# Rotary embedding on one core: unit 0 loaded by two DMA issuers instead of three, with 24 KB rows on GpSimd

## The chip, the cores and the metric

One core of a Trainium2 chip runs the whole kernel. The metric is the device time of one execution in microseconds (us). A profiled execution also has a span, from the first to the last recorded instruction, some 1.7 us shorter than the time. A run more than 1.5% above the fastest of its kernel is labelled slow.

## The reference

```python
# x: (8, 8, 1024, 64) fp32, freqs: (32,), positions: (1024,), scale = 0.5
angles = np.outer(positions * scale, freqs)
cos, sin = np.cos(angles), np.sin(angles)
x1, x2 = x[..., :32], x[..., 32:]
out = np.concatenate([x1 * cos - x2 * sin, x1 * sin + x2 * cos], axis=-1)
```

16.8 MB come in, 16.8 MB go out, and each output element takes two products and one sum or difference.

## The kernel before

The 64 heads are worked on in 4 units of 16 heads. A unit is a tile of 128 partitions with N = 8192 values each, so one partition's row is 32 KB of fp32 in HBM. In this kernel GpSimd's loads of x cast to fp16 on the way in; those from SyncE and ScalarE do not, so what they load goes into an fp32 tile X0f and ScalarE casts it. NH is N / 2.

```python
X0f = xout.tile([P, N], FP32, tag="O")
Q = NH // 2
pin(nc.sync.dma_start(out=X0f[:, :Q], in_=xv[0][:, NH : NH + Q]))      # third quarter, 8 KB rows

pin(nc.scalar.dma_start(out=pos_i64, in_=...))                         # 128 rows of 64 B
pin(nc.scalar.dma_start(out=freq_row, in_=freqs[None, :]))             # one row of 128 B
pin(nc.scalar.dma_start(out=X0f[:, Q:NH], in_=xv[0][:, NH + Q :]))     # last quarter, 8 KB rows
# ...
pin(nc.gpsimd.dma_start(out=Xf[0][:, :NH], in_=xv[0][:, :NH]))         # first half, 16 KB rows, cast
# ... (constants)
for u in range(1, NU):
    pin(nc.gpsimd.dma_start(out=Xf[u], in_=xv[u]))                     # 32 KB rows, cast
# ... (tables: cfreq and posf -> y -> r -> sine and cosine -> spread to T by TensorE,
#      copied from PSUM by VectorE and ScalarE)
pin(nc.scalar.copy(out=Xf[0][:, NH:], in_=X0f[:, :NH]))                # cast of SyncE's and ScalarE's half

for u in range(NU):
    OUT = xout.tile([P, N], FP32, tag="O")                             # 3 buffers
    for s in range(2):                                                 # two halves of a row
        # ...
        pin(nc.vector.tensor_tensor(out=pr, in0=Xs, in1=sin_b, op=ALU.mult))
        pin(nc.vector.tensor_tensor(out=Xs, in0=Xs, in1=cos_b, op=ALU.mult))
        # ... one subtract and one add on VectorE
        pin(nc.scalar.copy(out=OUT[:, ns], in_=Xf[u][:, ns]))
        if u in (0, NU - 1):
            eng = nc.gpsimd if (u, s) == (0, 1) else nc.sync
            pin(eng.dma_start(out=ov[u][:, ns], in_=OUT[:, ns]))       # half a unit
    if u not in (0, NU - 1):
        pin(nc.gpsimd.dma_start(out=ov[u], in_=OUT))                   # a whole unit
```

## Time and profile before

| | before |
|---|---|
| time, median of the first three runs | 84.3 us (84.08 to 84.32) |
| span of the profiled run | 82.7 us |
| VectorE busy / ScalarE busy | 73% / 49% |
| packets of all DMA queues, share of 16 engines | 96.7% |
| first packet / last packet ends | 1.74 / 81.40 us |

The DMA engines are shared by all queues, and each DMA is cut into one packet for each partition's row, 8 rows an engine. "Packet records" below are the trace's list of such packets, with start, duration and size. In the views q0 is GpSimd's queue, q1 SyncE's and q10 ScalarE's. A bracket at the end of a timeline line gives how long the engine had been idle and what ended the wait. A load has landed when its completion is signalled. The prediction shows the lines and how they are read.

### The profile page before, as it was taken

Reading aid. Unit: us, or ns where it says so; the run is one execution under the profiler, and the core shown is the slowest. Engines: PE = TensorE matmul, PEld = TensorE weight load, DVE = VectorE, ACT = ScalarE, POOL = GpSimd, SP = SyncE. Lnnn points to the kernel's source line nnn. Section 1 sums busy time; section 2 is a strip of 40 time slices with the busy share of each in tenths; the row PEclk is TensorE's granted clock in tenths of the full one; section 3 lists DMA queues with packets and bytes.
Section 4 is the critical chain, followed back from the end, with each engine's and each line's share of the span. In section 5 each row is a group of like instructions: output and inputs, shape, how many; then the busy total and the mean of one; then the engine's idle time right before and its main releaser. Section 6 shows DMA issues by size and latency. Waiting matters only on the chain.

```text
span 82.7 us, 179 instructions
## 1 busy us (share of the span) xinstructions
PE 6.5 (8%) x18; PEld 2.5 (3%) x18; DVE 60.3 (73%) x40; ACT 40.1 (49%) x18; POOL 5.2 (6%) x15
## 2 busy tenths in 40 slices
PE   0020898100000000000000000000000000000000
PEld 0020332000000000000000000000000000000000
DVE  0306376999999999999999999999999997000000
ACT  0603169999950790394098059209606902940000
POOL 4920000000000002000000200000200000000000
PEclk9999999997555555555555555555555555555555
DMA  2899997997997999799998999997999699699990
GB/s 56 328 319 281 285 345 167 254 246 151 238 254 143 238 285 317 285 278 333 262 222 174 278 468 396 507 507 317 444 507 460 301 507 492 285 468 396 436 444 16
DMA packets 1874, 26.22 MB, mean 317 GB/s; under 512 B 338, under 2 KB 338, under 8 KB 338
## 3 DMA queue, kind: packets, MB, share of 16 engines
q0 software_dynamic: 1008, 17.83, 72.0%
q1 hardware_dynamic: 576, 7.34, 21.5%
q10 hardware_dynamic: 290, 1.06, 3.2%
HBM read 16.79 MB, written 16.78 MB: 406 GB/s over the span
## 4 chain that ended last, share of the span: by engine, by line
DVE 55%; ACT 15%; DMA 5%; issue 5%; PE 5%; DVEq 1%; ACTq 0%
DVE X L154 20%; DVE pr L153 19%; DVE X L158 9%; DVE X L155 6%; ACT T L139 6%; DMA freq_row<-in_freqs_dram 5%; ACT OUT L161 4%; PE ps L129 4%; ACT X L140 4%; DVEq L195 1%; PE cfreq L97 1%; ACT tab L122 1%; DVE r L113 1%; DVE y L104 1%; ACTq L69 0%
## 5 line engine op out<-in xcount | busy, mean ns | idle before, releaser
L161 ACT CAST OUT<-X 128x4096 f32<-128x4096 f16 x8 | 28.8, 3606 | 24.2 <-DVE X L158 24.2
L153 DVE TENSOR_TENSOR pr<-X,T 128x4096 f16<-128x4096 f16 x8 | 18.3, 2292 | 1.0 <-ACT T L139 0.7
L154 DVE TENSOR_TENSOR X<-X,T 128x4096 f16<-128x4096 f16 x8 | 18.3, 2292 | 0.3
L155 DVE TENSOR_TENSOR X<-X,pr 128x2048 f16<-128x2048 f16 x8 | 9.8, 1225 | 0.3
L158 DVE TENSOR_TENSOR X<-pr,X 128x2048 f16<-128x2048 f16 x8 | 9.7, 1218 | 0.0
L139 ACT CAST T<-ps 128x1024 f16<-128x1024 f32 x6 | 5.7, 1028 | 2.6 <-PE ps L129 2.6
L129 PE MATMUL ps<-tab,sel 128*128 128x512 f16 x16 | 5.9, 529 | 2.6 <-ACT tab L122 2.2
L137 DVE CAST T<-ps 128x1024 f16<-128x1024 f32 x2 | 2.5, 1225 | 2.2 <-PE ps L129 2.2
L140 ACT CAST X<-X0f 128x4096 f16<-128x4096 f32 x1 | 3.6, 3650 | 0.0
L166 POOL DMA_DIRECT2D out_dram<-OUT x2 | 1.1, 533 | 27.1 <-ACT OUT L161 27.1
L95 DVE COPY sel<-one 128x2048 f16<-128x2048 f16 x1 | 0.7, 693 | 2.8 <-POOL one L87 2.8
L117 ACT ACTIVATE tab<-r 128x256 f16<-128x256 f32 x1 | 0.4, 417 | 4.2 <-DVE r L113 4.2
L117 ACT ACT_TABLE_LOAD x1 | 1.3, 1283 | 2.1 <-issue 2.1
L164 POOL DMA_DIRECT2D out_dram<-OUT x1 | 0.5, 543 | 26.7 <-ACT OUT L161 26.7
L129 PEld LDWEIGHTS <-sel 128*128 128x128 f16 x16 | 2.0, 126 | 6.0 <-issue 5.7
L92 POOL DMA_DIRECT2D X<-in_x_dram x3 | 2.0, 659 | 0.0
L100 DVE CAST posf<-pos_i 128x8 f32<-128x8 int32 x1 | 0.2, 172 | 2.3 <-DMA pos_i<-in_positions_dram 2.3
L97 PE MATMUL cfreq<-freq_row,coef 1*128 1x32 f32 x2 | 0.6, 392 | 5.7 <-DMA freq_row<-in_freqs_dram 5.7
L104 DVE TENSOR_TENSOR y<-posf,cfreq 128x256 f32<-128x256 f32 x1 | 0.4, 422 | 0.4 <-PE cfreq L97 0.4
L83 POOL DMA_DIRECT2D X<-in_x_dram x1 | 0.7, 669 | 0.8 <-POOLq L181 0.8
L97 PEld LDWEIGHTS cfreq<-freq_row,coef 1*128 1x128 f32 x2 | 0.5, 308 | 5.7 <-issue 5.7
L122 ACT ACTIVATE tab<-ra,quarter 128x256 f16<-128x256 f32 x1 | 0.5, 507 | 0.0
(11 smaller groups left out, 2.3 us busy)
## 6 DMA issues: line engine op xcount, KB each, us to landing
out_dram<-OUT POOLq DMA_DIRECT2D x2, 4096.0 KB, 14.9
X<-in_x_dram POOLq DMA_DIRECT2D x3, 2048.0 KB, 31.8
out_dram<-OUT SPq DMA_DIRECT2D x3, 2048.0 KB, 10.5
out_dram<-OUT POOLq DMA_DIRECT2D x1, 2048.0 KB, 21.1
X0f<-in_x_dram SPq DMA_DIRECT2D x1, 1024.0 KB, 4.8
X<-in_x_dram POOLq DMA_DIRECT2D x1, 1024.0 KB, 11.6
X0f<-in_x_dram ACTq DMA_DIRECT2D x1, 1024.0 KB, 12.1
pos_i<-in_positions_dram ACTq DMA_DIRECT2D x1, 8.0 KB, 5.0
```

Of the source, the lines that this page charges most:

```text
L92: pin(nc.gpsimd.dma_start(out=Xf[u], in_=xv[u]))
L97: nc.tensor.matmul(out=cfreq, lhsT=coef, rhs=freq_row, start=True, stop=True)
L117: pin(nc.scalar.activation(out=tab[:, 0], in_=r, func=AF.Sin, bias=0.0, scale=-_TWO_PI_DN))
L129: nc.tensor.matmul(out=ps[:, i].rearrange("p t w -> p (t w)"), lhsT=sel[:, g + i].rearrange("s h q -> s (h q)"), rhs=tab.rearrange("s t k ...
L137: pin(nc.vector.tensor_copy(out=dst, in_=ps))
L139: pin(nc.scalar.copy(out=dst, in_=ps))
L140: pin(nc.scalar.copy(out=Xf[0][:, NH:], in_=X0f[:, :NH]))
L153: pin(nc.vector.tensor_tensor(out=pr, in0=Xs, in1=sin_b, op=ALU.mult))
L154: pin(nc.vector.tensor_tensor(out=Xs, in0=Xs, in1=cos_b, op=ALU.mult))
L155: pin(nc.vector.tensor_tensor(out=Xs[:, :, 0, :], in0=Xs[:, :, 0, :], in1=pr[:, :, 1, :], op=ALU.subtract))
L158: pin(nc.vector.tensor_tensor(out=Xs[:, :, 1, :], in0=pr[:, :, 0, :], in1=Xs[:, :, 1, :], op=ALU.add))
L161: pin(nc.scalar.copy(out=OUT[:, ns], in_=Xf[u][:, ns]))
```

## The change

Its intent: to take bulk loading off ScalarE's queue, so that ScalarE issues only the two small loads, to halve ScalarE's cast, and to give GpSimd longer rows.

```diff
-    Q = NH // 2
-    pin(nc.sync.dma_start(out=X0f[:, :Q], in_=xv[0][:, NH : NH + Q]))
+    Q = N // 4
+    pin(nc.sync.dma_start(out=X0f[:, :Q], in_=xv[0][:, N - Q :]))
...
-    pin(nc.scalar.dma_start(out=X0f[:, Q:NH], in_=xv[0][:, NH + Q :]))
...
-    pin(nc.gpsimd.dma_start(out=Xf[0][:, :NH], in_=xv[0][:, :NH]))
+    pin(nc.gpsimd.dma_start(out=Xf[0][:, : N - Q], in_=xv[0][:, : N - Q]))
...
-    pin(nc.scalar.copy(out=Xf[0][:, NH:], in_=X0f[:, :NH]))
+    pin(nc.scalar.copy(out=Xf[0][:, N - Q :], in_=X0f[:, :Q]))
```

## The prediction

> **What bounds the kernel now.** I read the page first. Its part 1 has VectorE (DVE) as the busiest compute engine at 73%, and its part 4 follows the chain that ended last mostly through VectorE (55%). That is an invitation to count VectorE's waits. Three further lines speak against it:
>
> ```profile
> q0 software_dynamic: 1008, 17.83, 72.0%
> q1 hardware_dynamic: 576, 7.34, 21.5%
> q10 hardware_dynamic: 290, 1.06, 3.2%
> HBM read 16.79 MB, written 16.78 MB: 406 GB/s over the span
> ```
>
> The last column is the time that each queue's packets took, as a share of 16 DMA engines over the whole span. Summed it is 96.7% of 82.7 us, or 79.9 us. No other resource is near that. (The page's own 317 GB/s counts destination bytes, and a load that casts fp32 to fp16 writes half of what it reads; the 33.6 MB through HBM are the real load.)
>
> A mean share can hide gaps, so next comes the view by windows, cut where the DMA work changes. Columns: stretch and length, busy us of PE, PEld, DVE, ACT and POOL, the clock, DMA share, GB/s (destination bytes).
>
> ```profile
> 0.00:1.74 1.74, 0.00 (x0) 0.00 (x0) 0.00 (x0) 0.00 (x0) 0.69 (x5) 1.00 0.00 0
> 1.74:4.70 2.96, 0.00 (x0) 0.00 (x0) 0.69 (x1) 1.28 (x1) 2.86 (x8) 1.00 0.99 346
> 4.70:12.60 7.90, 4.66 (x12) 2.03 (x13) 4.06 (x7) 2.36 (x4) 0.00 (x0) 1.00 1.12 301
> 12.60:22.00 9.40, 1.80 (x7) 0.48 (x5) 8.59 (x5) 9.40 (x7) 0.00 (x0) 0.87 0.99 211
> ...
> 61.50:71.50 10.00, 0.00 (x0) 0.00 (x0) 8.05 (x5) 5.42 (x2) 0.00 (x0) 0.50 1.00 431
> 71.50:81.40 9.90, 0.00 (x0) 0.00 (x0) 0.00 (x0) 1.79 (x1) 0.00 (x0) 0.50 0.93 399
> 81.40:82.70 1.30, 0.00 (x0) 0.00 (x0) 0.00 (x0) 0.00 (x0) 0.00 (x0) 0.50 0.00 0
> ```
>
> The DMA share is about 1 in every stretch between 1.74 and 81.4 (packets are booked where they start, so it wobbles around 1). I also added up the packet records over time: from 4 us to 80 us no stretch of 2 us has less than 15.98 of 16 engines at work. VectorE, on the other hand, does nothing in the last 10 us. The span is therefore three pieces: 1.74 us until the first packet, 79.7 us of packets without a gap, 1.25 us until the last store is confirmed.
>
> How much slack has the compute chain against that? From the timeline and the chain of waits:
>
> ```profile
> 66.31 7.33 SPq L164 DMA_DIRECT2D out_dram<-OUT  x2
> 69.69 3.60 ACT OUT L161
> ```
>
> ScalarE writes the last half output until 73.3, and SyncE starts issuing its store then. By the packet records that store's first packet starts at 75.92, straight behind the last packet of the store before it on the same queue. On an empty queue SyncE's first load took 1.0 us from issue (0.74) to first packet (1.74), so the last store could have started at 74.3. The chain through VectorE and ScalarE is thus some 1.6 us early (an estimate from these two numbers). **The bound is the DMA engines**; the chain in part 4 is only the longest chain of instructions.
>
> **What the Trainium skill says.** "DMA: Bandwidth & Descriptors", section "Issuing engines are not separate DMA queues", says that DMAs started by ScalarE, SyncE or GpSimd all end up on the same 16 DMA engines and interleave. The trace agrees: alone, SyncE's 8 KB rows take 309 ns each; while ScalarE's 8 KB rows and GpSimd's 16 KB rows are both under way, one of each takes 924 ns on an engine, the sum of the two plus about 10 ns. The same page, section "SWDGE vs HWDGE vs iDMA", says that only a DMA from GpSimd can cast. That is why the rows that leave ScalarE's queue also change from fp32 plus a ScalarE cast to a cast in flight. "Perfetto Trace Analysis", section "What 'DMA-bound' means", asks which DMA resource binds: here it is the engines and not an issuing sequencer, whose issues take 0.35 to 0.9 us each. The first page's section "Where 436 GB/s comes from" gives a ceiling of about 435 GB/s; the 33.6 MB in 79.7 us are 421 GB/s, so there is little left to gain from any arrangement of the same bytes.
>
> **The change part by part.** Unit 0 is 128 rows (partitions) of 32 KB in HBM.
>
> ```profile
> 1.25 0.67 POOL L83 DMA_DIRECT2D X<-in_x_dram  x1 [0.81 <-POOLq L181]
> 1.74 0.35 ACTq L72 DMA_DIRECT2D X0f<-in_x_dram  x1
> 13.20 2.29 DVE L153 TENSOR_TENSOR pr<-X,T 128x4096 f16<-128x4096 f16 x1 [0.67 <-ACT T L139]
> 16.68 3.65 ACT L140 CAST X<-X0f 128x4096 f16<-128x4096 f32 x1
> 20.36 2.29 DVE L153 TENSOR_TENSOR pr<-X,T 128x4096 f16<-128x4096 f16 x1 [0.15 <-ACT X L140]
> ...
> X0f<-in_x_dram SPq DMA_DIRECT2D x1, 1024.0 KB, 4.8
> X<-in_x_dram POOLq DMA_DIRECT2D x1, 1024.0 KB, 11.6
> X0f<-in_x_dram ACTq DMA_DIRECT2D x1, 1024.0 KB, 12.1
> ```
>
> *SyncE's load.* Q is 2048 before and after (a quarter of a row, 8 KB). SyncE only takes another quarter, the last instead of the third. Cost and time to landing stay at 4.8 us.
>
> *Bytes on the DMA engines.* HBM bytes do not change. Removed: 128 rows of 8 KB (ScalarE) and 128 of 16 KB (GpSimd); added: 128 of 24 KB (GpSimd). Each engine has 8 of each. Before: 8 x 924 ns = 7.39 us. After: a 16 KB row alone took 605 ns (first GpSimd row at 4.72, first ScalarE row behind it at 5.325) and a 32 KB row of the later units 1208 ns from start to start; halfway between, 24 KB is 906 ns, so 8 x 906 = 7.25 us. The saving is **0.14 us**, on the bound.
>
> *When unit 0 lands.* Before, GpSimd's half landed at 1.25 + 11.6 = 12.85, about 0.54 after its last packet (12.31). Now three quarters land together: packets that ended at 12.61 end 0.14 earlier, at 12.47, and with 0.54 for completion the landing is at about **13.0**. VectorE's first product waits until 13.18 for the tables T, the copy by ScalarE that the trace names. So it should still start near 13.2, with only 0.2 us to spare.
>
> *ScalarE's cast.* L140 shrinks from 4096 to 2048 elements a row: 3.65 to about 1.83 us. It follows the table copies, so it ends near 18.5 instead of 20.33, and VectorE's second half starts when it is free, at 20.23 instead of 20.36: 0.13 us off the compute chain. The other 1.7 us become idle time of ScalarE, because its next work (L161) waits for VectorE at 20.24 either way.
>
> *ScalarE's issue.* One issue of 0.35 us goes; the table load behind it moves up to about 1.75. It had over 4 us to spare before the first sine at 7.59. The two small loads ahead of it are issued as before, and frequencies that land at 5.6 still start the tables.
>
> Sum: the compute chain is about 0.13 us shorter and the DMA stream about 0.14 us shorter. As they lie beside each other, I take the stream: 84.3 - 0.14 = 84.16, put at **84.2 us**.
>
> **The rivals.** (1) *The first product waits for the longer load.* If the single completion for three quarters comes after 13.18, VectorE starts late by the difference. For it: the margin is 0.2 us, and the half of the data that the first product needs is no longer announced on its own. Against a cost: the chain has about 1.6 us to spare at its end, so a landing up to about 14.7 costs nothing; beyond that, each microsecond costs one. Only a landing over 3 us late would reach 2%. (2) *ScalarE's relief pays.* If the chain of part 4 were the bound and the cast on it (4.2% of the span), one would expect up to 1.8 us, so 82.5. Against it: VectorE waited only 0.15 us for this cast, and the stores drain at full rate until 81.4. (3) *Long GpSimd rows run badly*, or delay the small frequency row because a 0.9 us packet gets in front of it. For it: that row's packet (4.84) is near GpSimd's first (4.72). Against it: 32 KB rows already run at 27.1 bytes per ns and engine, as fast as any; a delayed frequency row would cost the chain at most one packet, 0.9 us, inside its slack. A bad row rate of 10% would cost 0.7 us, 85.0. (4) *A hole in the stream*: with one queue fewer at the start an engine might run dry. Against it: GpSimd's queue alone holds share 0.99 between 12.6 and 22.
>
> **Range and chances.** Everything that I can put a number on lies within 0.2 us, and three runs before spread by 0.24. So 83.9 to 84.5 should hold it 8 times in 10; the longer side of what may go wrong is slower. Two per cent is 1.7 us. Faster by that would need bytes to vanish (chance 0.01); slower would need a landing 3 us late or a much worse row rate (0.02); within 2%: 0.97.
>
> **What would show it right or wrong.** Right: DMA shares still sum to 96 to 97% of the span; GpSimd's first load lands about 11.7 us after its issue; VectorE's first product at about 13.2, waiting for T; the L140 cast at 1.8 us and no wait of VectorE for it; the end still 1.2 us after the last packet, with the last store queued behind the one before it. Wrong: a first product waiting on the DMA of X well beyond 13.2, a stretch after 1.74 us with a DMA share well below 1, 24 KB rows far from 906 ns, or an end that follows the last ScalarE cast directly.

## The result, and the profile after

| | before | after |
|---|---|---|
| time, median of 6 runs | 84.27 us (84.08 to 84.33) | 84.17 us (84.08 to 84.44) |
| ratio | | 0.9997, 95% interval 0.9977 to 1.0016 |

A ratio compares the fast runs of both kernels in the same rounds, so it is not quite the ratio of the medians. The profiled run after happened to be the longest of its six (84.44).

First the page after, DMA queues: packets, MB written at the destination, share of 16 engines.

```profile
q0 software_dynamic: 1008, 18.35, 75.3%
q1 hardware_dynamic: 576, 7.34, 21.5%
q10 hardware_dynamic: 146, 0.01, 0.1%
```

ScalarE's queue q10 has given its 3.2% to GpSimd's queue q0. The sum is 96.9%, as full as before. The view by windows, the same columns as in the prediction:

```profile
1.74:4.70 2.96, 0.00 (x0) 0.00 (x0) 0.69 (x1) 1.28 (x1) 2.86 (x8) 1.00 0.98 337
4.70:12.60 7.90, 4.46 (x12) 1.98 (x13) 3.94 (x7) 2.17 (x4) 0.00 (x0) 1.00 1.12 240
...
71.50:81.40 9.90, 0.00 (x0) 0.00 (x0) 0.00 (x0) 1.94 (x1) 0.00 (x0) 0.50 0.96 410
```

The DMA share is near 1 again to the end, with VectorE idle in the last stretch. The fall from 301 to 240 GB/s between 4.7 and 12.6 is no loss: more of the load is cast, and these are destination bytes. By the packet records the 24 KB rows follow each other at 907 ns on an engine (926 ns each, overlapping a little), where a pair of a 16 KB and an 8 KB row took 924 ns before.

The timeline and the DMA issues of unit 0:

```profile
13.39 2.29 DVE L152 TENSOR_TENSOR pr<-X,T 128x4096 f16<-128x4096 f16 x1 [0.67 <-ACT T L138]
16.87 1.94 ACT L139 CAST X<-X0f 128x2048 f16<-128x2048 f32 x1
20.51 2.29 DVE L152 TENSOR_TENSOR pr<-X,T 128x4096 f16<-128x4096 f16 x1
...
X<-in_x_dram POOLq DMA_DIRECT2D x1, 1536.0 KB, 11.4
X0f<-in_x_dram SPq DMA_DIRECT2D x1, 1024.0 KB, 4.7
```

Three quarters of unit 0 now land together at 1.25 + 11.4 = 12.65. The first product still waits for the tables and not for this load. The cast is 1.7 us shorter (1.94 instead of 3.65), and the bracket that told VectorE's wait of 0.15 us for it is gone. All of ScalarE's gain became its idle time: its wait for VectorE rose from 24.2 to 25.8 us in the sum of the output casts.

The tables came 0.2 us later in this profile, since TensorE got the frequencies at 5.91 instead of 5.71. That is not an effect of the change: other profiles of the same lines have 5.59 to 5.77 (below).

### The profile page after: what moved, and what is told of

Same layout as the page of the kernel before. It is cut to its first block, busy times and chain, and to the rows that moved or that the text cites. A ratio compares the mean times of both kernels' runs of the same rounds, so it can differ in the third digit from the quotient of the medians.

```text
span 82.7 us, 177 instructions
## 1 busy us (share of the span) xinstructions
PE 6.7 (8%) x18; PEld 2.7 (3%) x18; DVE 60.3 (73%) x40; ACT 38.5 (47%) x18; POOL 5.2 (6%) x15
## 4 chain that ended last, share of the span: by engine, by line
DVE 64%; ACT 7%; DMA 6%; issue 5%; PE 5%; DVEq 1%; ACTq 0%
DVE X L153 22%; DVE pr L152 22%; DVE X L157 10%; DVE X L154 8%; DMA freq_row<-in_freqs_dram 6%; ACT OUT L160 4%; PE ps L128 4%; DVEq L194 1%; ACT T L138 1%; PE cfreq L96 1%; ACT tab L121 1%; DVE r L112 1%; DVE y L103 1%; ACTq L69 0%; ACT tab L116 0%
## 5 line engine op out<-in xcount | busy, mean ns | idle before, releaser
L160 ACT CAST OUT<-X 128x4096 f32<-128x4096 f16 x8 | 28.8, 3606 | 25.8 <-DVE X L157 25.8
L139 ACT CAST X<-X0f 128x2048 f16<-128x2048 f32 x1 | 1.9, 1942 | 0.0
## 6 DMA issues: line engine op xcount, KB each, us to landing
X<-in_x_dram POOLq DMA_DIRECT2D x1, 1536.0 KB, 11.4
```

Of the source, the lines that this page charges most:

```text
L139: pin(nc.scalar.copy(out=Xf[0][:, N - Q :], in_=X0f[:, :Q]))
```

## The experiments

Two theories. **A**: the DMA engines are the bound; the chain through VectorE and ScalarE ends with time to spare. **B**: that chain sets the end, and the DMA is full only because there is always something to store. All runs start from the changed kernel; ratios are against the kernel before in the same rounds. All results are correct except where a store is cut short.

### The changed kernel again

No edit.

> The changed kernel once more. Both theories: 84.1 to 84.3, ratio to before 0.998 to 1.000 if the 0.14 us saved on the DMA stream survive, 1.000 if they do not. In the profile: rows of 24 KB 907 ns from start to start, first load of GpSimd landing 11.4 us after issue. Open: whether the frequency row is again 0.2 us later than before (5.9 against 5.7).

Measured: 84.22 us (84.03 to 84.56), ratio 0.9992, interval 0.9969 to 1.0014. The 24 KB rows are at 907 ns again and their load lands at 1.25 + 11.5 = 12.75. The frequencies reach TensorE at 5.59, so the 0.2 us of the first profile was scatter. Whether the 0.14 us saved in unit 0 reach the end is below the resolution: they would be 0.17%, and the interval is 0.22% to each side. The packet records show where they drown. In the profile after, unit 1's rows ended 0.15 us earlier than before (22.16 against 22.31), and in the eight profiles that have the changed loads they ended between 22.02 and 22.26. Unit 3's, loaded while SyncE's first store runs among them, ended between 47.08 and 47.62 in these eight (47.27 before).

### VectorE delayed near the end, by a little and by much

```diff
             pin(nc.vector.tensor_tensor(out=pr, in0=Xs, in1=sin_b, op=ALU.mult))
+            if (u, s) == (3, 0):          # a_late1: half a product more
+                h = KH // 2
+                pin(nc.vector.tensor_tensor(out=pr[:, :h], in0=Xs[:, :h], in1=sin_b[:, :h], op=ALU.mult))
```

In a_late5 two whole products stand there instead.

> Half a product more on VectorE at the start of unit 3, idempotent, 1.17 us. Theory A (the DMA stream is the bound, the compute chain has about 1.6 us to spare at the last store): 84.2, no change. Theory B (the chain through VectorE and ScalarE sets the end): 85.3.

Measured: 84.40 us, ratio 1.0003, interval 0.998 to 1.0027. A microsecond of VectorE costs nothing that the time resolves (0.3% is 0.2 us).

> Two whole products more on VectorE at the start of unit 3, 4.6 us. Theory A: 4.6 less the slack of 1.6 to 1.7, so 87.1 (3.0 us slower), with a hole in the DMA stream before the last store. Theory B: 88.8.

Measured: 87.16 us, ratio 1.0334, against 84.32 before: 2.84 us slower for 4.66 us (two repeats of 2.33) of delay, so 1.8 us of slack at the last store. (By the spans, 85.0 to 85.2 against 82.3 to 82.8, the slack would be nearer 2.1 us: in this kernel alone the time is 2.0 us longer than the span and not 1.7 to 1.8, and no run says why.) The windows of that run show the hole between the last two stores:

```profile
71.50:76.50 5.00, 0.00 (x0) 0.00 (x0) 2.67 (x3) 2.27 (x1) 0.00 (x0) 0.50 0.99 419
76.50:78.70 2.20, 0.00 (x0) 0.00 (x0) 0.00 (x0) 1.34 (x1) 0.00 (x0) 0.50 0.02 7
78.70:83.80 5.10, 0.00 (x0) 0.00 (x0) 0.00 (x0) 0.00 (x0) 0.00 (x0) 0.50 0.96 408
```

B falls with these two: it asked for 85.3 and 88.8.

### The same small delay, one unit earlier

The edit of a_late1 with (2, 0) instead of (3, 0).

> The same 1.17 us as in a_late1, but at the start of unit 2, so that GpSimd's store of unit 2 is issued later too (at 60.8 instead of 59.64, while its first packet was at 61.6). Theory A with a GpSimd store that needs 1.0 us from issue to first packet: 84.2 to 84.5. If it needs the whole 1.95 us seen, the slack is nil there: 85.3 and a hole of 1.2 us at 61.6. Theory B: 85.3 too, but without a hole.

Measured: 84.46 us, ratio 1.0011, interval 0.9988 to 1.0035. The time does not tell it from no change, but the trace does. The windows before and inside a short hole (a window counts packets by their starts):

```profile
51.50:61.20 9.70, 0.00 (x0) 0.00 (x0) 9.56 (x6) 5.41 (x2) 0.53 (x1) 0.50 1.00 432
...
61.30:61.70 0.40, 0.00 (x0) 0.00 (x0) 0.37 (x2) 0.00 (x0) 0.00 (x0) 0.50 0.02 0
```

GpSimd issued unit 2's store at 60.64, 1.2 us later than in a_late1, and its first packet came at 61.74, 1.1 us after that. The share of 0.02 alone proves no hole, since rows of unit 1's store that had started before still ran until 61.65. Added up by starts and ends, the packet records show 0.3 us of the 16 engines' time lost here, where a_late1 lost none, and the first packet came 0.37 us later than in a_late1 (61.37). So the slack at unit 2's store is about 0.8 us, half of that at the last store.

### Less to store

Two kernels that are wrong: a_less_tail leaves out a quarter of the row of the store before the last, a_less_mid half of the row of unit 1's store.

```diff
+                if (u, s) == (3, 0):                       # a_less_tail
+                    ns = slice(0, NH - NH // 4)
                 pin(eng.dma_start(out=ov[u][:, ns], in_=OUT[:, ns]))
-            pin(nc.gpsimd.dma_start(out=ov[u], in_=OUT))
+            w = N - N // 2 if u == 1 else N                # a_less_mid
+            pin(nc.gpsimd.dma_start(out=ov[u][:, :w], in_=OUT[:, :w]))
```

> Wrong on purpose: a quarter of the second last store (unit 3, first half) is left out, 4 KB of each row, 8 x 151 ns = 1.2 us of the DMA stream; no instruction of VectorE or ScalarE changes. Theory A: 83.0 (the 1.2 us are under the slack of 1.6 to 1.7). Theory B: 84.2, as the chain is the same.

Measured: 82.95 us against 84.25 before, ratio 0.9837 (0.9808 to 0.9865). Removing 1.2 us of packets removed 1.3 us of time, while no compute instruction changed.

> Wrong on purpose: half of unit 1's store (16 KB of each row, 8 x 605 ns = 4.8 us of the stream) is left out. Theory A, with the slack that a_mid1 showed at unit 2's store (about 0.8 us: 1.17 us late left a hole of 0.33 us): the gain is cut to 0.8 us, 83.4, and a hole of 4 us stands in the stream before unit 2's store. If the slack were the 1.6 us of the last store: 82.6. Theory B: 84.2.

Measured: 83.23 us against 84.12, ratio 0.9921 (0.9866 to 0.9976); three runs at 83.2 to 83.3 and one at 84.2. Of 4.8 us of packets some 0.9 us came through; the rest is a hole before unit 2's store, 3.8 us of the 16 engines' time by the packet records:

```profile
57.10:60.50 3.40, 0.00 (x0) 0.00 (x0) 3.33 (x3) 2.06 (x1) 0.53 (x1) 0.50 0.00 0
60.50:70.50 10.00, 0.00 (x0) 0.00 (x0) 9.01 (x6) 4.46 (x2) 0.00 (x0) 0.50 1.04 446
```

Unit 2's store could not start before 60.55, against 61.37 in a_late1's profile: 0.8 us, the slack that a_mid1 had shown.

### ScalarE's cast made as long as before

```diff
     pin(nc.scalar.copy(out=Xf[0][:, N - Q :], in_=X0f[:, :Q]))
+    pin(nc.scalar.copy(out=Xf[0][:, N - Q :], in_=X0f[:, :Q]))
```

> ScalarE does its cast of X0f twice (idempotent), so that it is busy as long as before the change: 3.9 us. Theory A: VectorE waits 0.1 to 0.3 us for it, 84.2. If ScalarE's relief were worth its length: 86.1.

Measured: 84.26 us, ratio 1.0016, interval 0.9998 to 1.0033. The timeline:

```profile
18.59 1.90 ACT L140 CAST X<-X0f 128x2048 f16<-128x2048 f32 x1
20.40 3.60 ACT L161 CAST OUT<-X 128x4096 f32<-128x4096 f16 x1
20.52 2.29 DVE L153 TENSOR_TENSOR pr<-X,T 128x4096 f16<-128x4096 f16 x1 [0.37 <-ACT X L140]
```

VectorE waits 0.37 us for the cast, inside the slack. ScalarE's relief of 1.7 us is worth nothing that the time resolves.

### Another share for SyncE: an eighth, nothing, a half

`Q = N // 8` in a_eighth; in a_whole the load of SyncE and the cast are removed and GpSimd loads all of unit 0; `Q = N // 2` in a_half.

> SyncE loads only the last eighth of unit 0, GpSimd seven eighths. Theory A: SyncE's packets end near 3.4, GpSimd's first packet comes at 4.7, so the engines are idle for about 1.4 us and the time is 85.5. Theory B: VectorE's first product waits for GpSimd's load at 4.72 + 8 x 1057 ns + 0.25 = 13.4, as now; ScalarE's cast is 1 us shorter: 84.2 or a little less.

Measured: 84.26 us, ratio 1.0007, interval 0.9962 to 1.0052. A's number was wrong. There is no hole, because GpSimd's first row came at 3.50, not at 4.7. I had read 4.7 as GpSimd's own start-up; it was a wait behind SyncE's rows. The first product was now late, at 13.68, since GpSimd's load landed at 1.25 + 12.3 = 13.55, and that too cost nothing that the time resolves:

```profile
13.68 2.29 DVE L152 TENSOR_TENSOR pr<-X,T 128x4096 f16<-128x4096 f16 x1 [2.54 <-ACT T L138]
```

The bracket names a copy of the tables, which had long been written; the load is what landed last.

> GpSimd loads all of unit 0, no load by SyncE, no cast by ScalarE. Theory A: the stream starts at 4.7 instead of 1.75, minus nothing: 87.1. Theory B: unit 0 lands at 4.72 + 8 x 1208 ns + 0.25 = 14.6, 1.3 us after the tables: 85.4.

Measured: 85.02 us, ratio 1.0084 (1.0052 to 1.0115). Both numbers were off for the same reason: with no SyncE load at all, GpSimd's first row came at 2.63. The windows at the start, and the first product:

```profile
1.70:2.60 0.90, 0.11 (x1) 0.14 (x1) 0.00 (x0) 0.89 (x1) 0.82 (x5) 1.00 0.09 9
2.60:12.60 10.00, 6.30 (x18) 2.31 (x18) 4.67 (x8) 5.42 (x8) 2.06 (x4) 1.00 1.05 210
...
13.94 2.29 DVE L148 TENSOR_TENSOR pr<-X,T 128x4096 f16<-128x4096 f16 x1 [4.08 <-DMA X<-in_x_dram]
```

The stream starts 0.88 us late and the time is 0.7 to 0.85 us longer. VectorE starts 0.7 us late as well, so this run alone would not separate A from B; the packets of the last stores still follow each other without a gap, which is A's mark. SyncE's early load is worth these 0.7 to 0.85 us.

> SyncE loads half of unit 0 in one DMA of 16 KB rows, GpSimd the other half; ScalarE loads no x but casts 4096 elements a row again (3.65 us). Theory A: same bytes, no hole: 84.2. Theory B with ScalarE's cast on the path: as before the change, 84.3, VectorE waiting 0.1 to 0.2 us for the cast.

Measured: 88.96 us, ratio 1.0512 (1.0437 to 1.0587). A large miss of both theories. Its profile fell on a run labelled slow (89.37, which is 1.5% above the kernel's fastest, 88.05); the fast runs, 88.05 to 89.33, are all at least 3.8 us slower than before, and the profiled run's clock (0.63) is as theirs. The timeline:

```profile
10.67 0.17 DVE L99 CAST posf<-pos_i 128x8 f32<-128x8 int32 x1 [7.18 <-DMA pos_i<-in_positions_dram]
11.74 0.60 PE L96 MATMUL cfreq<-freq_row,coef 1*128 1x32 f32 x2 [11.74 <-DMA freq_row<-in_freqs_dram]
19.22 2.29 DVE L152 TENSOR_TENSOR pr<-X,T 128x4096 f16<-128x4096 f16 x1 [0.67 <-ACT T L138]
```

The two small loads landed 5 to 6 us late, the tables followed, and the first product started at 19.22 instead of 13.2. That is 6 us, far over the slack, and the DMA share is 0.00 from 62.4 to 66.6, once more before unit 2's store. Added up, the records show 4.3 us of the engines' time lost there and 0.7 us before unit 1's store. The 64 B rows of the positions ran from 2.86 to 9.54 and ended with SyncE's 16 KB rows (1.76 to 9.54). In the changed kernel they end with SyncE's 8 KB rows too (5.12).

### Is it SyncE's row size or SyncE's bytes?

```diff
-    Q = N // 4
-    pin(nc.sync.dma_start(out=X0f[:, :Q], in_=xv[0][:, N - Q :]))
+    Q = N // 2
+    h = Q // 2
+    pin(nc.sync.dma_start(out=X0f[:, :h], in_=xv[0][:, N - Q : N - h]))
+    pin(nc.sync.dma_start(out=X0f[:, h:Q], in_=xv[0][:, N - h :]))
```

> SyncE loads the same half of unit 0 as in a_half, but as two DMAs of 8 KB rows instead of one of 16 KB rows. In a_half (4.7 us slower) the positions landed at 10.7 and the frequencies at 11.7 us instead of 5.7, and the tables came 6 us late. Theory C (on each DMA engine the 64 B rows of ScalarE's small loads alternate one for one with SyncE's rows, so SyncE's row size sets when they land): positions at 5.7 to 6.0 again, first product at 13.2 to 13.5, time 84.2. Theory D (the small loads wait until SyncE's bytes are through, or 2 MB ahead of them are simply too much): as a_half, first product near 19, 88 to 89.

Measured: 84.10 us, ratio 1.0000 (0.9985 to 1.0014).

```profile
5.64 0.60 PE L98 MATMUL cfreq<-freq_row,coef 1*128 1x32 f32 x2 [5.64 <-DMA freq_row<-in_freqs_dram]
5.78 0.17 DVE L101 CAST posf<-pos_i 128x8 f32<-128x8 int32 x1 [2.30 <-DMA pos_i<-in_positions_dram]
13.13 2.29 DVE L154 TENSOR_TENSOR pr<-X,T 128x4096 f16<-128x4096 f16 x1 [0.67 <-ACT T L140]
```

The same 2 MB on the same queue, in rows of half the size, cost nothing. Theory D falls, and the size of SyncE's first eight rows an engine is what sets when the small loads land. Every load of SyncE here has eight rows an engine, so the times alone do not part the row's size from the whole first load's; the packet records do, with one 64 B row an engine after each of SyncE's rows (every 0.31 us in the changed kernel, every 0.61 us at first in a_half).

The next run asks whether the turns really alternate. In a_freq1st ScalarE issues the frequencies first and the positions second.

> ScalarE issues the frequency row ahead of the positions. Theory C: the frequencies then take their turn after the first row of SyncE and land before 4 us; the positions still need eight turns and land at 5.7 to 6.2, so the tables start within 0.4 us of now. Theory A: whatever it is, 84.2, for the chain has slack.

Measured: 84.31 us, ratio 1.0019 (0.9998 to 1.0039), with one slow run, 85.45, on which the profile fell. In that profile SyncE's rows run from 1.75 to 5.01, much as in the fast runs (1.75 to 5.12 in the profile after).

```profile
2.17 0.63 PE L96 MATMUL cfreq<-freq_row,coef 1*128 1x32 f32 x2 [2.17 <-POOL quarter L84]
5.63 0.17 DVE L99 CAST posf<-pos_i 128x8 f32<-128x8 int32 x1 [2.13 <-DMA pos_i<-in_positions_dram]
```

The frequencies had arrived before TensorE was ready for them at 2.17, and the positions by 5.63. The times are near Theory C's, but not by its mechanism: the frequency row went out at 1.62, before SyncE's first row and not after it. The positions, issued 0.55 us later than otherwise, took no turns between SyncE's rows: all their packets lie between 4.75 and 5.07, when SyncE's were almost through. Alternation is what the packets show when both loads are issued at once; a load issued a little later waits behind rows that the engines seem to have taken in already. What rule joins the two stays open.

## Why the prediction was right

*The bound.* Right, and tested from both sides: 1.2 us less to store gave 1.3 us, while 1.2 us more on VectorE gave nothing that the time resolves. After the change, too, the last store's first packet (76.13) came right behind the last rows of the store before it, and the end 1.2 us after the last packet (81.44). No run separates the 16 engines from the memory behind them as what sets the rate of a row. Part 4 of the page, which follows waits between instructions, could not show this; the sum of the queues' shares could.

*The saving of 0.14 us.* Its term is right: 907 ns for each 24 KB row where 906 was worked out, and unit 1's loads ended 0.15 us earlier. At the end of the kernel it is not resolved, and I do not claim it for the time; that the median came to 84.17 where 84.16 was worked out is luck within a spread of 0.36 us.

*Unit 0's landing.* 12.65 instead of the 13.0 expected. I had taken 0.54 us from last packet to landing from the kernel before; here it was 0.25. The records show what I misread: the load ends with 16 packets of 4 B, and before the change these took turns with ScalarE's last rows, the last of them at 12.61, 0.24 us before the landing. The tables of that profile were ready at 13.37, so the margin was 0.7 us and not 0.2; in a_again, with 12.75 against 13.06, it was 0.3.

*ScalarE's cast.* 1.94 us where 1.83 was estimated by halving, and VectorE's wait for it gone, as expected. a_cast2 shows that nothing was to be had there.

*The slack, the mis-sized term.* "The chain is some 1.6 us early" holds for the last store (1.8 measured; in a_late5 that store needed 0.8 us and not 1.0 from issue at 77.87 to first packet at 78.70). But a delay at the start of the kernel, the only one that this change could cause, also delays unit 2's store, and there only 0.8 us are free. (Unit 1's store, though earlier, has more: in a_half 6 us of delay left a hole of 0.7 us there.) The rival's sentence that a landing "up to about 14.7 costs nothing" should have said about 14.0, and a frequency row 0.9 us late was just outside the slack, not inside. With a landing at 12.65 to 12.75 it made no difference; in a_half it was the measure of the loss (6.0 us late less 0.8 is 5.2; the runs were 3.8 to 5.1 us slower).

*The small loads.* The prediction said that they "are issued as before" and took that for enough. That it held is luck: the change left SyncE's rows at 8 KB. With rows of 16 KB the neighbour would have lost 4.7 us, more than any of my four rivals allowed.

No version beat the kernels. The best, a_half_8k at ratio 1.0000, has the same stream; with 1.74 us before the first packet, 33.6 MB at 421 GB/s and 1.25 us of completion, the span is spent, and no run here shortened one of these pieces without leaving out bytes.

## What to carry to other kernels

Add up the DMA queues' shares before believing the chain of instructions; when they fill the span, moving bytes from one queue to another has little to gain (0.14 us here by the rows, not resolved in the time), though it can cost (4.7 us in a_half), and an engine freed by it only waits longer. Slack is a number for each store: look at each place where the delayed chain feeds the stream for the one with the least, not at the end alone. When a bulk load and a small urgent load were issued together here, the bulk load's row size decided when the small one landed; it is worth trying short first rows.

## What the Trainium skill lacked or had wrong

- "DMA: Bandwidth & Descriptors", section "Queues, rings and completion order", says that an engine round-robins between the queue rows it has work for, at packet granularity, with about 9 to 17 descriptors to a packet. Loads issued together took turns here (positions from 2.86 to 9.54 among SyncE's 16 KB rows), but after every single record of the trace, one row each; and the positions issued 0.55 us later sent nothing until 4.75, when SyncE's eight rows an engine were almost through. The page lacks this wait behind another queue's rows. It shows for GpSimd too: its first row came 1.4 us after the start of its issue with no SyncE rows ahead, 2.25 us with 4 KB rows ahead, 3.5 us with 8 KB rows and 4.3 us with 16 KB rows, in the last case with 48 of SyncE's 128 rows still to start, so it is not always a wait for the whole load; and SyncE's first store of unit 3 went from issue at 66.31 to first packet at 71.05.
- The same page, section "Where 436 GB/s comes from", says that for transfers between HBM and SBUF the HBM side, about 358 GB/s a core, binds. This core moved 33.6 MB in 79.7 us, 421 GB/s. Taken alone the sentence misleads. The page's own measurement of 425 GB/s, with the pair's other core idle, fits better; what the other core did here is not recorded.
- "Perfetto Trace Analysis", section "Identifying the Most-Contended Engine", advises HBM utilization instead of occupancy for DMA, because 16 engines make occupancy misleading. The packet time summed over the 16 engines, 96.7% of the span, was the reading that found the bound. The advised figure would have pointed the same way: 406 GB/s over the span is 113% of the 358 GB/s above.
